# The dense expert stage in groups of four parts, two PSUM banks per operation, tokens innermost in the weights

## The chip, the core and the metric

The kernel runs on one core of a Trainium2 chip. Its engines are named as in the profile: PE multiplies matrices (PEld is its loading of the stationary operand), DVE is the vector engine, ACT the scalar engine, POOL is GpSimd, and SP issues transfers to the DMA queues. The metric is the device time of one execution in microseconds (us). One profiled execution of each kernel is looked at by the instruction; the timed runs are others.

## The reference

One layer of a streaming encoder for 1088 tokens (1024 of a prompt, 64 of a sample): three branches (an mLSTM, a gating unit, a cross-attention) are merged, and then comes a table of 16384 experts, of which every token takes 128. This last part is where the change lies:

```
def _peer(xn, w_pq, k_sub1, k_sub2, u_exp, v_exp):
    ...
        q = (xb @ w_pq).reshape(PEER_BLOCK, PEER_HEADS, PEER_DQ)
        s1 = jnp.einsum('thd,kd->thk', q[..., :half], k_sub1)
        s2 = jnp.einsum('thd,kd->thk', q[..., half:], k_sub2)
        v1, i1 = lax.top_k(s1, PEER_TOPK)
        v2, i2 = lax.top_k(s2, PEER_TOPK)
        ...
        sc, pos = lax.top_k(cand, PEER_TOPK)
        e = jnp.take_along_axis(cidx, pos, axis=-1).reshape(PEER_BLOCK, PEER_HEADS * PEER_TOPK)
        g = jax.nn.softmax(sc, axis=-1).reshape(PEER_BLOCK, PEER_HEADS * PEER_TOPK)
        a = jax.nn.gelu(jnp.einsum('tkd,td->tk', u_exp[e], xb))
        return jnp.einsum('tk,tkd->td', (g * a).astype(xb.dtype), v_exp[e])
```

Each row of `u_exp` and `v_exp` has 1024 numbers. A token's output is the sum, over its 128 experts, of weight x gelu(u . x) x v. The result is normalised (RMSNorm) and written out.

## The kernel before, in words

The 1088 tokens are nine tiles of up to 128 rows: 0 to 7 and "s". For tiles 0, 1, "s", 6 and 7 the experts are **gathered**: for each of the 128 places of a token, POOL issues one indirect DMA (L1018) that fetches one row of `u_exp` for each of 128 tokens (512 KB); DVE multiplies and sums it with the tokens (L1031, "a u row" below); the same for `v_exp` (L1039, "a v row"). There are 3 buffers for u rows and 4 for v rows (`BU, BV = 3, 4`). A gather is issued when its buffer is free, and a buffer is free when DVE has used the row ahead in it.

For tiles 2 to 5 (512 tokens, `TD`) all 16384 experts are computed **densely**. This has three stages:

- *Lookahead* (`ahead`): the four tiles are transposed to `dxh`, `dxl`, and the first `LG` = 6 parts of the hidden layer are made. A part is 256 experts: `hidden(m)` makes x . u for them and 512 tokens (L1093 to L1095, three matmuls for each product, since every operand is split in a high and a low fp32r half), and ACT puts gelu of it into `ge` (L1099).
- *Hot stage* (`dense`, L1168 to L1190): the table of weights, one number for each token and expert, is made by products of one-hot matrices, four tokens at a time: DVE compares (L1168) and multiplies (L1172), ACT scales one part of it (L1177), PE multiplies (L1181), ACT copies the 512 x 128 numbers from PSUM to a staging tile `sg` (L1183), and every 32 tokens `sg` is stored to `gd` in DRAM (L1190). Then the signal "weights" lets the selection for tiles 6 and 7 start.
- *Outer stage*: 32 steps of 512 experts. `weigh` multiplies four `ge` tiles with a piece of the weights `g4`, loaded from `gd` (L1203, L1210), casts the product to its high half (ACT, L1211) and subtracts for the low half (L1212). `outer` multiplies them with `v_exp`, 512 of 1024 columns at a time (L1223 to L1225), four PSUM banks for the four token tiles, and DVE adds each bank to `ob` in SBUF (L1229). Between the two halves of a step `hidden` runs for a part that is `LG` parts ahead.

The weights `u_exp`, `v_exp` stream through a ring: SP loads 512 KB pieces, ACT casts 512 columns to the high half (L277, in `w_split`) and DVE subtracts for the low half (L280, "a split" below). Each split serves 12 matmuls of 512 columns, in `hidden` and in `outer` alike, and is made up to four ahead (`HL` = 4).

The parts are written as Python generators, "streams", each of which yields an estimate of its cost or waits for a signal; `Flow.run` takes the stream whose sum of costs is least, and this sets the order of the code. A scheduler then sets the order on each engine. The engines run their own order strictly.

## Time and profile before

| | |
|---|---|
| timed runs | 3677.53, 3679.82, 3681.61 us (median 3679.82) |
| the profiled execution, its own time | 3696.64 us |
| its span, first to last instruction | 3694.7 us |
| PE, PEld | 3267.0 us (88%), 2635.0 us (71%) |
| DVE | 3228.9 us (87%) |
| ACT, POOL | 1381.8 us (37%), 1701.9 us (46%) |
| DMA | 1024.81 MB, 277 GB/s over the span |

A share is that of the engine's busy time in the whole span. PE's and DVE's are near each other, and a mean over the span does not say which of them waits for the other in a given stretch; the rows further down are therefore taken by stretch, in us from the start of the span.

### The profile page before, as it was taken

Reading aid. Unit: us, or ns where it says so; the run is one execution under the profiler, and the core shown is the slowest. Engines: PE = TensorE matmul, PEld = TensorE weight load, DVE = VectorE, ACT = ScalarE, POOL = GpSimd, SP = SyncE. Lnnn points to the kernel's source line nnn. Section 1 sums busy time; section 2 is a strip of 40 time slices with the busy share of each in tenths; the row PEclk is TensorE's granted clock in tenths of the full one; section 3 lists DMA queues with packets and bytes.
Section 4 is the critical chain, followed back from the end, with each engine's and each line's share of the span. In section 5 each row is a group of like instructions: output and inputs, shape, how many; then the busy total and the mean of one; then the engine's idle time right before and its main releaser. Section 6 shows DMA issues by size and latency. Waiting matters only on the chain.

```text
span 3694.7 us, 46871 instructions
## 1 busy us (share of the span) xinstructions
PE 3267.0 (88%) x15364; PEld 2635.0 (71%) x15364; DVE 3228.9 (87%) x6811; ACT 1381.8 (37%) x2671; POOL 1701.9 (46%) x1208
## 2 busy tenths in 40 slices
PE   8999998899986497599867876899999999999998
PEld 6787876576675365477756766677778888888886
DVE  5556797768989999998999899998889999999997
ACT  5555533423333143233324555332223333333332
POOL 1001334447856775654431472344345565545651
PEclk9999998899998698799978867999999999999999
DMA  7445467789897787897876797788889999999995
GB/s 231 146 163 187 158 240 253 252 278 332 320 361 277 265 300 266 287 318 270 280 256 206 232 282 238 265 286 296 294 304 354 354 350 348 344 322 317 346 338 180
DMA packets 447440, 1024.81 MB, mean 277 GB/s; under 512 B 32182, under 2 KB 169566, under 8 KB 443100
## 3 DMA queue, kind: packets, MB, share of 16 engines
q0 software_dynamic: 166528, 604.58, 46.5%
q1 hardware_dynamic: 276828, 413.06, 33.8%
q10 hardware_dynamic: 3840, 4.20, 0.4%
q8 instruction: 120, 1.97, 0.2%
q14 instruction: 124, 1.02, 0.1%
HBM read 968.44 MB, written 53.26 MB: 277 GB/s over the span
## 4 chain that ended last, share of the span: by engine, by line
PE 31%; DVE 9%; issue 7%; POOL 3%; DMA 2%; ACT 0%; DVEq 0%; POOLq 0%; ACTq 0%; SPq 0%
PE po L1225 4%; PE po L1224 4%; PE po L1223 4%; PE ph L1095 4%; PE ph L1094 4%; PE ph L1093 4%; POOL gu L1018 3%; PE po L1181 2%; DVE gacc L1039 2%; DMA gu<-in_u_exp_dram,e 1%; DVE wl L280 1%; DVE gu L1031 1%; DVE one L1172 1%; DVE ge L1210 0%; DVE one L1168 0%
## 5 line engine op out<-in xcount | busy, mean ns | idle before, releaser
L1018 POOL DMA_INDIRECT gv<-in_v_exp_dram,e x522 | 826.9, 1584 | 670.6 <-DVE gacc L1039 349.6
L1018 POOL DMA_INDIRECT gu<-in_u_exp_dram,e x576 | 746.1, 1295 | 833.5 <-DVE gu L1031 509.3
L277 ACT CAST wh<-wraw 128x512 fp32r<-128x512 f32 x994 | 612.8, 621 | 1249.6 <-PE acc L313 390.2
L1031 DVE SCALAR_TENSOR_TENSOR gu<-gu,gx 128x1024 f32<-128x1024 f32 x576 | 699.8, 1217 | 157.0 <-DMA gu<-in_u_exp_dram,e 153.2
L280 DVE TENSOR_TENSOR wl<-wraw,wh 128x512 fp32r<-128x512 f32 x962 | 651.1, 684 | 150.7 <-ACT wh L277 147.9
L1039 DVE SCALAR_TENSOR_TENSOR gacc<-gv,w,gacc 128x1024 f32<-128x1024 f32 x448 | 571.0, 1274 | 25.4 <-DMA gv<-in_v_exp_dram,e 24.1
L312 PE MATMUL acc<-wl,half 128*128 128x512 f32 (+1 forms) x1152 | 477.5, 415 | 8.3 <-DVE wl L280 8.3
L313 PE MATMUL acc<-wh,half 128*128 128x512 f32 (+1 forms) x1152 | 458.9, 404 | 0.0
L311 PE MATMUL acc<-wh,half 128*128 128x512 f32 (+1 forms) x1152 | 417.1, 413 | 6.4 <-ACT uB L470 2.6
L1224 PE MATMUL po<-wl,W 128*128 128x512 f32 x1024 | 402.4, 393 | 12.2 <-DVE wl L280 12.0
L1095 PE MATMUL ph<-dxh,wl 128*128 128x512 f32 x1024 | 393.2, 394 | 12.8 <-DVE wl L280 12.6
L1094 PE MATMUL ph<-dxl,wh 128*128 128x512 f32 x1024 | 399.7, 390 | 1.3 <-DVE dxl L1118 1.3
L1225 PE MATMUL po<-wh,W 128*128 128x512 f32 x1024 | 399.3, 391 | 0.5 <-DVE W L1212 0.5
L1093 PE MATMUL ph<-dxh,wh 128*128 128x512 f32 x1024 | 399.5, 390 | 0.2 <-ACT dxh L1117 0.2
L1223 PE MATMUL po<-wh,W 128*128 128x512 f32 x1024 | 352.4, 391 | 23.8 <-ACT W L1211 20.6
L328 PE MATMUL acc<-half,wh 128*128 128x256 f32 (+2 forms) x768 | 253.8, 350 | 18.8 <-ACT wh L277 12.5
L311 PEld LDWEIGHTS acc<-wh,half 128*128 128x128 f32 (+1 forms) x1152 | 211.8, 185 | 78.4 <-issue 15.8
L312 PEld LDWEIGHTS acc<-wl,half 128*128 128x128 f32 (+1 forms) x1152 | 214.2, 186 | 74.5 <-issue 11.4
L329 PE MATMUL acc<-half,wh 128*128 128x256 f32 (+2 forms) x768 | 261.9, 346 | 0.0
L313 PEld LDWEIGHTS acc<-wh,half 128*128 128x128 f32 (+1 forms) x1152 | 212.8, 186 | 54.7 <-issue 1.5
L330 PE MATMUL acc<-half,wl 128*128 128x256 f32 (+2 forms) x768 | 226.9, 342 | 14.7 <-DVE wl L280 14.5
L1223 PEld LDWEIGHTS po<-wh,W 128*128 128x128 f32 x1024 | 192.8, 188 | 66.0 <-ACT W L1211 20.9
(444 smaller groups left out, 5233.3 us busy)
## 6 DMA issues: line engine op xcount, KB each, us to landing
wraw<-in_w_in_dram SPq DMA_DIRECT2D x216, 512.0 KB
wraw<-in_v_exp_dram SPq DMA_DIRECT2D x125, 512.0 KB
wraw<-in_u_exp_t_dram SPq DMA_DIRECT2D x68, 512.0 KB
gd<-sg SPq DMA_DIRECT2D x16, 2048.0 KB
g<-gd SPq DMA_DIRECT2D x32, 1024.0 KB
wrawx<-in_u_exp_t_dram SPq DMA_DIRECT2D x60, 512.0 KB
wraw<-in_w_pq_dram SPq DMA_DIRECT2D x48, 512.0 KB
wraw<-in_w_out_dram SPq DMA_DIRECT2D x24, 512.0 KB
```

The costliest lines, as they stand in the source:

```text
L277: S.copy(h, t)
L280: E.tensor_tensor(l, t, h.bitcast(F32), op=ALU.subtract)
L311: T.matmul(ps[i], xh[:, cs], h, start=(k == 0), stop=False)
L312: T.matmul(ps[i], xh[:, cs], l, start=False, stop=False)
L313: T.matmul(ps[i], xl[:, cs], h, start=False, stop=(last and b is None))
L1018: G.indirect_dma_start(out=tl, out_offset=None, in_=src, in_offset=bass.IndirectOffsetOnAxis(ap=col, axis=0))
L1031: V.scalar_tensor_tensor(tl, tl, 1.0, xn, op0=ALU.mult, op1=ALU.mult, accum_out=av[:, j:j + 1])
L1039: V.scalar_tensor_tensor(x2, gt_.pop(op), st_v[t][1][:, j:j + 1], x2, op0=ALU.mult, op1=ALU.add)
L1093: T.matmul(o, h[:, cs], xh[:, k + kk, :], start=(k + kk == 0), stop=False)
L1094: T.matmul(o, h[:, cs], xl[:, k + kk, :], start=False, stop=False)
L1223: T.matmul(o, w_[:, k, cs], h, start=(k == 0), stop=False)
L1224: T.matmul(o, w_[:, k, cs], l, start=False, stop=False)
```

## The change

The constants `SC`, `NS`, `NH` go; a part is 256 experts (`NP` = 64 of them), four parts are a group (`GP` = 4), and the lookahead `LG` is 4 parts in place of 6. A PSUM tile has two banks, and one operation works on both: gelu, product, cast, subtraction and add have 1024 elements to a partition in place of 512. The outer products of four parts (1024 experts, in place of 512) are summed in PSUM ahead of one add, so 64 adds of 1024 take the place of 256 of 512. The product with the weights is made right behind each part's hidden layer (`times_g`), not all at the step's start, and `g4` is loaded after every second one into one buffer. In `gd`, `sg` and `g4` tokens are innermost, 32 in a row, in place of four experts; for this the two operands of the hot matmul change places, and one copy of 1024 elements moves 8 tokens, reading PSUM with 128 numbers between elements. `sg` lives in a pool of its own (`hp`), whose place the five `W` buffers (`vp`) take afterwards. The numbers of matmuls, splits and gathers and the bytes moved are the same. Lines of after: product L1092, hidden L1108 to L1110, equality and product L1187, L1191, hot matmul L1200, subtraction L1229, outer L1258 to L1260, add L1269.

```diff
-    gd = dram.tile([32, 128, TD, 4], F32, name="gd")
+    gd = dram.tile([32, 128, TD // 32, 4, 32], F32, name="gd")
...
-    SC = 4
-    NS = NEXP // (128 * SC)
-    LG = 6
-    NH = 4
+
+    NP = NEXP // 256
+    GP = 4
+    LG = 4
...
+    def two_banks():
+        return ps_d.tile([128, 2, 512], F32, name="po", bufs=2)
...
+    g4s = {}
+    def load_g(s_):
+        if 2 * s_ < NP:
+            g4s[s_] = dp.tile([128, TD // 32, 4, 32], F32, name="g4")
+            SP.dma_start(g4s[s_], gd[s_])
+    def times_g(m):
+        ge = st["ge", m].rearrange("p c (b t) -> p c b t", t=32)
+        g4 = g4s[m // 2].rearrange("p b c t -> p c b t")
+        V.tensor_tensor(ge, ge, g4[:, m % 2 * 2:m % 2 * 2 + 2], op=ALU.mult)
+        if m % 2:
+            g4s.pop(m // 2)
+            load_g(m // 2 + 1)
     def hidden(m):
-        if m >= 2 * NS:
+        if m >= NP:
             return
         xh, xl = st["dx"]
-        ps = [psd("ph", NH) for _ in range(2)]
+        ps = ps_d.tile([128, 2, 512], F32, name="ph", bufs=2)
         for k in range(0, KD, 2):
             h, l = w_get()
             for kk in range(2):
                 for c in range(2):
                     cs = slice(kk * 256 + c * 128, kk * 256 + c * 128 + 128)
-                    o = ps[c][:, 0:TD]
+                    o = ps[:, c, 0:TD]
                     T.matmul(o, h[:, cs], xh[:, k + kk, :], start=(k + kk == 0), stop=False)
                     T.matmul(o, h[:, cs], xl[:, k + kk, :], start=False, stop=False)
                     T.matmul(o, l[:, cs], xh[:, k + kk, :], start=False, stop=(k + kk == KD - 1))
-            yield 12 * 0.217 * TD / 512
-        for c in range(2):
-            ge = dp.tile([128, TD], F32, name="ge", bufs=2 * LG)
-            S.activation(ge, ps[c][:, 0:TD], AF.Gelu_apprx_tanh)
-            st["ge", 2 * m + c] = ge
+            yield 12 * 0.233 * TD / 512
+        ge = dp.tile([128, 2, TD], F32, name="ge", bufs=LG)
+        S.activation(ge, ps[:, :, 0:TD], AF.Gelu_apprx_tanh)
+        st["ge", m] = ge
...
-            x = dp.tile([128, D], F32, name="dxn", tag="W", bufs=2)[0:n]
+            x = dp.tile([128, D], F32, name="dxn", tag="ge", bufs=LG)[0:n]
...
-                sg = dp.tile([128, 32, 32, 4], F32, name="sg", tag="W", bufs=2)
...
+                sg = hp.tile([128, 32, 4, 32], F32, name="sg", bufs=2)
+                for t1 in range(0, 32, 8):
+                    p = two_banks()
+                    for b in range(2):
+                        tb = t0 + t1 + 4 * b
+                        ts = slice(tb, tb + 4)
+                        eq, pr = hots[tb // 4 % len(hots)]
+                        V.tensor_tensor(eq, io[:, None].to_broadcast([128, 2, 128, 4]),
+                                        kb[:, :, None, ts].to_broadcast([128, 2, 128, 4]), op=ALU.is_equal)
+
+                        nd = 2 + b
+                        V.tensor_tensor(pr[:, 0:nd], eq[:, 0, None].to_broadcast([128, nd, 128, 4]),
+                                        gb[:, 0:nd, None, ts].to_broadcast([128, nd, 128, 4]), op=ALU.mult)
+                        for j in range(nd, 3):
+                            for t2 in range(4):
+                                S.activation(pr[:, j, :, t2], eq[:, 0, :, t2], AF.Copy,
+                                             scale=gf_[:, tb + t2:tb + t2 + 1])
+
                         for t2 in range(4):
...
-                    S.copy(sg[:, :, t1:t1 + 4, :].rearrange("p g t c -> p t g c"),
-                           p.rearrange("p (t g c) -> p t g c", t=4, c=4))
-                    yield 0.7
+                            for j in range(3):
+                                T.matmul(p[:, b, t2 * 128:(t2 + 1) * 128], eq[:, 1, :, t2], pr[:, j, :, t2],
+                                         start=(j == 0), stop=(j == 2))
+                        yield 0.5
+                    S.copy(sg[:, :, :, t1:t1 + 8].rearrange("p g c t -> p (g c) t"),
+                           p.rearrange("p b (t e) -> p e (b t)", t=4))
+                    yield 0.4
                 nd1 += 32
                 if nd1 == TD:
-                    st["weights"] = sg
+                    st["weights"] = tok = kp.tile([128, 1], F32, name="tok")
+                    V.tensor_copy(tok, sg[:, 0, 0, 0:1])
                     fl.signal("weights")
-                SP.dma_start(gd[:, :, t0:t0 + 32, :].rearrange("g p t c -> p g (t c)"),
-                             sg.rearrange("p g t c -> p g (t c)"))
+                SP.dma_start(gd[:, :, t0 // 32].rearrange("g p c t -> p g (c t)"),
+                             sg.rearrange("p g c t -> p g (c t)"))
...
+        W_ = {}
+        def weigh(m):
+            if m >= NP:
+                return
+            w_ = vp.tile([128, 2, 2, TD], F32R, name="W", bufs=GP + 1)
+            ge = st.pop(("ge", m))
+            S.copy(w_[:, 0], ge)
+            V.tensor_tensor(w_[:, 1], ge, w_[:, 0].bitcast(F32), op=ALU.subtract)
+            W_[m] = w_
         load_g(0)
-        w_ = weigh(0)
+        for m in range(LG):
+            times_g(m)
+            weigh(m)
         gfin = None
         ss = dp.tile([128, 2, ND], F32, name="dss")
         V.memset(ss, 1.0)
...
+        for g in range(NP // GP):
+            last = g == NP // GP - 1
+            for j in range(2 * GP):
+                hf, q = divmod(j, GP)
+                m = GP * g + q
+                if j % 2 == 0 and GP * g + j // 2 + LG < NP:
+                    mh = GP * g + j // 2 + LG
+                    yield from hidden(mh)
+                    times_g(mh)
+                if j == 0:
+                    weigh(GP * g + LG)
+                if q == 0:
+                    ps = [two_banks() for _ in range(ND // 2)]
+                w_ = W_[m]
+                for k in range(2):
+                    h, l = w_get()
+                    for i in range(ND):
+                        o, cs = ps[i // 2][:, i % 2], slice(i * 128, i * 128 + 128)
+                        hi, lo = w_[:, 0, k, cs], w_[:, 1, k, cs]
+                        T.matmul(o, hi, h, start=(q == 0 and k == 0), stop=False)
+                        T.matmul(o, hi, l, start=False, stop=False)
+                        T.matmul(o, lo, h, start=False, stop=(q == GP - 1 and k == 1))
+                    yield 0.7 * ND
+                if hf:
+                    W_.pop(m)
+                    if q < GP - 1:
+                        weigh(GP * g + LG + q + 1)
+                if q == GP - 1:
+                    for i in range(ND // 2):
+                        o = ob[:, 2 * i:2 * i + 2, hf * 512:(hf + 1) * 512]
+                        V.tensor_tensor(o, o, ps[i], op=ALU.add)
```

How the order moves on the engines, at three places. PE, in the middle of the hot stage, where the last hidden matmul of the lookahead stands (`ph` the PSUM tile, `po` that of the hot products, `hot` a one-hot buffer). Before:

```order
L1093 MATMUL ph_19546<-dxh_16576,wh_19547 128x512
L1094 MATMUL ph_19546<-dxl_16577,wh_19547 128x512
L1095 MATMUL ph_19546<-dxh_16576,wl_19548 128x512
L1181 LDWEIGHTS hot_16690
L1181 MATMUL po_17275<-hot_16690 128x128
```

After:

```order
L1108 MATMUL ph_19271<-dxh_16576,wh_19272 128x512
L1109 MATMUL ph_19271<-dxl_16577,wh_19272 128x512
L1110 MATMUL ph_19271<-dxh_16576,wl_19273 128x512
L1200 LDWEIGHTS hot_16692
L1200 MATMUL po_17072<-hot_16692 128x128
```

Ahead of the first outer matmul PE's order has 336 hidden matmuls before (seven parts of 48, the seventh from the loop) and 240 after (five parts).

DVE, where the outer stage starts (`g_19526`, `g_19247` are the loads of the weights, `cand` and `scv` belong to the selection for tile 7). Before:

```order
L857 TENSOR_TENSOR cand<-v_15774 128x8x8
L1210 TENSOR_TENSOR ge<-ge,g_19526 128x512 x4
L857 TENSOR_TENSOR cand<-v_15774 128x8x10
L857 TENSOR_TENSOR cand<-v_15774 128x8x12
L857 TENSOR_TENSOR cand<-v_15774 128x8x8
L981 COPY gx_22592<-gacc 64x1024
L1212 TENSOR_TENSOR W<-ge,W 128x512 x3
L799 MAX scv<-cand 128x8 x2
L1031 SCALAR_TENSOR_TENSOR gu,av<-gu,gx 128x1024
L799 MAX scv<-cand 128x8
```

After:

```order
L1092 TENSOR_TENSOR ge<-ge,g_19247 128x1024 x2
L897 TENSOR_TENSOR ei<-ei,oh 128x256
L1229 TENSOR_TENSOR W<-ge,W 128x1024
L906 SCALAR_TENSOR_TENSOR e<-ei 128x128
L857 TENSOR_TENSOR cand<-v_15774 128x8x16
L857 TENSOR_TENSOR cand<-v_15774 128x8x8
L857 TENSOR_TENSOR cand<-v_15774 128x8x10
L857 TENSOR_TENSOR cand<-v_15774 128x8x12
L857 TENSOR_TENSOR cand<-v_15774 128x8x8
L1229 TENSOR_TENSOR W<-ge,W 128x1024
L981 COPY gx_22009<-gacc 64x1024
L799 MAX scv<-cand 128x8 x8
L1092 TENSOR_TENSOR ge<-ge,g_19254 128x1024 x2
```

The products come in pairs of twice the size; the second pair, of the second load, stands 10 rows behind the first.

DVE further on, in the stretch of tile 6's u rows. Before:

```order
L1229 TENSOR_TENSOR ob<-ob,po 128x512 x4
L280 TENSOR_TENSOR wl<-wraw,wh 128x512
L1031 SCALAR_TENSOR_TENSOR gu,av<-gu,gx 128x1024
L280 TENSOR_TENSOR wl<-wraw,wh 128x512
L1031 SCALAR_TENSOR_TENSOR gu,av<-gu,gx 128x1024 x2
L280 TENSOR_TENSOR wl<-wraw,wh 128x512 x2
L1031 SCALAR_TENSOR_TENSOR gu,av<-gu,gx 128x1024
L1210 TENSOR_TENSOR ge<-ge,g_21750 128x512
L1031 SCALAR_TENSOR_TENSOR gu,av<-gu,gx 128x1024
L280 TENSOR_TENSOR wl<-wraw,wh 128x512
L1210 TENSOR_TENSOR ge<-ge,g_21750 128x512
L280 TENSOR_TENSOR wl<-wrawx,wh 128x512
```

After:

```order
L280 TENSOR_TENSOR wl<-wraw,wh 128x512
L1031 SCALAR_TENSOR_TENSOR gu,av<-gu,gx 128x1024
L280 TENSOR_TENSOR wl<-wraw,wh 128x512
L1092 TENSOR_TENSOR ge<-ge,g_20914 128x1024
L1031 SCALAR_TENSOR_TENSOR gu,av<-gu,gx 128x1024
L280 TENSOR_TENSOR wl<-wrawx,wh 128x512
L1031 SCALAR_TENSOR_TENSOR gu,av<-gu,gx 128x1024
L280 TENSOR_TENSOR wl<-wrawx,wh 128x512
L1031 SCALAR_TENSOR_TENSOR gu,av<-gu,gx 128x1024
L280 TENSOR_TENSOR wl<-wraw,wh 128x512
L1269 TENSOR_TENSOR ob<-ob,po 128x2x512 x2
L1031 SCALAR_TENSOR_TENSOR gu,av<-gu,gx 128x1024
```

Four adds of one bank in a row become two of two banks, in every second step, and one product of 1024 takes the place of two. Counted from the first product on, the 34th u row stands behind 43 splits before and behind 39 after; the 128th behind 132 and behind 120. Up to the 34th there are 24 products, 16 subtractions and 20 adds before, and 9, 9 and 4 after. From the first to the last equality operation of the hot stage there are 24 splits before and 17 after, and 64 v rows in both.

## Rows read from the trace of the kernel before

**Rows 1.** The profile page, part 1: busy time of each engine, its share of the span, and its instructions.

```profile
PE 3267.0 (88%) x15364; PEld 2635.0 (71%) x15364; DVE 3228.9 (87%) x6811; ACT 1381.8 (37%) x2671; POOL 1701.9 (46%) x1208
```

**Rows 2.** Busy time of each engine in four stretches. Columns: the stretch in us, its length, then busy us (and instructions) of PE, PE's weight loads, DVE, ACT and POOL, the granted TensorE clock, the share of the DMA engines, GB/s.

```profile
2150.00:2200.00 50.00, 34.25 (x275) 30.62 (x274) 49.08 (x64) 28.12 (x69) 36.01 (x16) 0.63 0.87 276
2550.00:2600.00 50.00, 47.39 (x204) 37.54 (x203) 43.20 (x70) 14.28 (x25) 20.60 (x18) 1.00 0.87 297
2900.00:2950.00 50.00, 50.00 (x223) 41.40 (x222) 50.00 (x70) 15.17 (x26) 29.22 (x23) 1.00 0.98 355
3655.00:3668.00 13.00, 13.00 (x59) 10.78 (x58) 8.01 (x22) 3.49 (x6) 0.00 (x0) 1.00 0.37 135
```

**Rows 3.** The timeline of PE, at two places of the dense stage: start, length, engine, line, instruction, out<-in. Each row is one matmul of 512 columns; rows between are left out.

```profile
3449.53 0.39 PE L1093 MATMUL ph<-dxh,wh 128*128 128x512 f32 x1
...
3450.43 0.39 PE L1094 MATMUL ph<-dxl,wh 128*128 128x512 f32 x1
...
3655.41 0.39 PE L1223 MATMUL po<-wh,W 128*128 128x512 f32 x1
...
3656.09 0.39 PE L1223 MATMUL po<-wh,W 128*128 128x512 f32 x1
```

**Rows 4.** PE's instructions by line from 2317.7 us to 3682 us: count, busy us, mean ns, and the idle time before them with what ended it.

```profile
L1093 PE MATMUL ph<-dxh,wh 128*128 128x512 f32 x912 | 355.8, 390 | 0.0
...
L1223 PE MATMUL po<-wh,W 128*128 128x512 f32 x1024 | 352.4, 391 | 23.8 <-ACT W L1211 20.6 <-DVE ob L1229 3.1
```

**Rows 5.** The timeline where the outer products begin (SPq is the queue that issues transfers on SyncE).

```profile
2297.14 0.58 ACT L1183 COPY sg<-po 128x512 f32<-128x512 f32 x1 [0.83 <-PE po L1181]
...
2297.75 0.40 SPq L1190 DMA_DIRECT2D gd<-sg  x1
...
2310.91 0.32 SPq L1203 DMA_DIRECT2D g<-gd  x1
...
2315.97 3.07 DVE L1210 TENSOR_TENSOR ge<-ge,g 128x512 f32<-128x512 f32 x3 [3.17 <-DMA g<-gd]
...
2317.74 0.80 PE L1223 MATMUL po<-wh,W 128*128 128x512 f32 x1 [20.63 <-ACT W L1211]
```

**Rows 6.** The timeline at the last outer matmul.

```profile
3681.02 0.39 PE L1225 MATMUL po<-wh,W 128*128 128x512 f32 x1
```

**Rows 7.** The waits from 2360 to 2760 us: engine and line, what it waited for, total us, times, longest.

```profile
POOL gu L1018 <- DVE gu L1031: 204.8, 111, 7.0
...
DVE gu L1031 <- DMA gu<-in_u_exp_dram,e: 43.4, 43, 3.2
...
PE ph L1095 <- DVE wl L280: 11.7, 16, 2.2
```

**Rows 8.** The timeline of DVE: the 34th gathered row of tile 6 (2450.90), a product and the split behind it, a split, the 128th row (2720.14) and the split behind it.

```profile
2450.90 1.22 DVE L1031 SCALAR_TENSOR_TENSOR gu<-gu,gx 128x1024 f32<-128x1024 f32 x1
...
2560.49 1.09 DVE L1210 TENSOR_TENSOR ge<-ge,g 128x512 f32<-128x512 f32 x1
2561.49 0.69 DVE L280 TENSOR_TENSOR wl<-wraw,wh 128x512 fp32r<-128x512 f32 x1
...
2719.54 0.69 DVE L280 TENSOR_TENSOR wl<-wraw,wh 128x512 fp32r<-128x512 f32 x1
2720.14 1.22 DVE L1031 SCALAR_TENSOR_TENSOR gu<-gu,gx 128x1024 f32<-128x1024 f32 x1
...
2721.29 0.69 DVE L280 TENSOR_TENSOR wl<-wraw,wh 128x512 fp32r<-128x512 f32 x1
```

**Rows 9.** DMA issues of the u gathers, from 2450 to 2700 us and from 500 to 700 us: count, and median us from issue to landing.

```profile
gu<-in_u_exp_dram,e POOLq DMA_INDIRECT x86, 6.5
...
gu<-in_u_exp_dram,e POOLq DMA_INDIRECT x74, 5.6
```

**Rows 10.** DVE's instructions by line from 2450.8 to 2721.28 us.

```profile
L1031 DVE SCALAR_TENSOR_TENSOR gu<-gu,gx 128x1024 f32<-128x1024 f32 x95 | 115.8, 1221 | 37.3 <-DMA gu<-in_u_exp_dram,e 36.6
```

**Rows 11.** The same from 500 to 700 us.

```profile
L1031 DVE SCALAR_TENSOR_TENSOR gu<-gu,gx 128x1024 f32<-128x1024 f32 x74 | 90.2, 1220 | 41.0 <-DMA gu<-in_u_exp_dram,e 40.9
```

**Rows 12.** The timeline of the hot stage: the last hidden matmul of the lookahead, the 33rd equality operation, four scaled copies of ACT, the last product.

```profile
2083.28 0.40 PE L1095 MATMUL ph<-dxh,wl 128*128 128x512 f32 x1
...
2101.03 0.68 DVE L1168 TENSOR_TENSOR hot<-one 128x1024 bf16<-128x1024 bf16 x1
...
2291.97 1.48 ACT L1177 ACTIVATE one<-one,hot 128x128 bf16<-128x128 bf16 x4
...
2293.78 0.95 DVE L1172 TENSOR_TENSOR gu<-gu,one 128x1536 bf16<-128x1536 bf16 x1
```

**Rows 13.** DVE's instructions by line from 1990 to 2101 us.

```profile
L1168 DVE TENSOR_TENSOR one<-one 128x1024 bf16<-128x1024 bf16 x16 | 11.0, 689 | 6.1 <-PE po L1181 6.1
...
L1168 DVE TENSOR_TENSOR gu<-one 128x1024 bf16<-128x1024 bf16 x8 | 5.5, 690 | 2.9 <-PE po L1181 2.9
```

**Rows 14.** ACT's instructions by line from 2100 to 2250 us.

```profile
L1183 ACT COPY sg<-po 128x512 f32<-128x512 f32 x65 | 40.1, 620 | 30.9 <-PE po L1181 30.7
```

**Rows 15.** DVE's instructions by line from 2315.9 to 2450.9 us.

```profile
L1031 DVE SCALAR_TENSOR_TENSOR gu<-gu,gx 128x1024 f32<-128x1024 f32 x34 | 41.1, 1213 | 3.7 <-DMA gu<-in_u_exp_dram,e 3.7
L1210 DVE TENSOR_TENSOR ge<-ge,g 128x512 f32<-128x512 f32 x24 | 24.9, 1066 | 3.2 <-DMA g<-gd 3.2
L280 DVE TENSOR_TENSOR wl<-wraw,wh 128x512 fp32r<-128x512 f32 x31 | 20.9, 680 | 0.0
```

More of the change, by code (lines that the diff above doesn't have):

```diff
@@ L611, in tile_stream_step @@
         want_u(m)
-    for m in range(2 * NS):
-        want_u(m + LG)
-        s_, hf = divmod(m, 2)
-        for r in range(2):
-            e0 = s_ * 128 * SC + 256 * r
+    for g in range(NP // GP):
+        for j in range(2 * GP):
+            if j % 2 == 0:
+                want_u(GP * g + j // 2 + LG)
+            hf, q = divmod(j, GP)
+            e0 = (GP * g + q) * 256
             pieces.append(a["v_exp"][e0:e0 + 256, hf * 512:(hf + 1) * 512].rearrange("(k p) c -> p k c", p=128))
@@ L1126, in dense @@
         yield "dx"
+        hot = ExitStack()
+        hp = hot.enter_context(tc.tile_pool(name="hp", bufs=1))
         one = dp.tile([128, 5 * TD + 512 + 2 * 2560], BF, name="one", tag="ob")
@@ L1131, in dense @@
         io = one[:, 5 * TD:5 * TD + 512].rearrange("p (c t) -> p c t", t=4)
[L1132 removed]
+        ioi = hp.tile([128, 128, 4], I32, name="ioi", tag="sg", bufs=2)
         G.iota(ioi, pattern=[[1, 128], [0, 4]], base=0, channel_multiplier=0)
@@ L1192, in dense @@
         yield "ahead"
+        hot.close()
+        vp = pool("vp", 1)
         ob = dp.tile([128, ND, D], F32, name="ob")
@@ L1197, in dense @@
             SP.dma_start(ob[0:n, i, :], x2d[t])
-        gs = {}
-        def load_g(s_):
-            if s_ < NS:
-                gs[s_] = dp.tile([128, TD, 4], F32, name="g4")
-                SP.dma_start(gs[s_], gd[s_])
-        def weigh(s_):
-            w_ = dp.tile([128, SC, 2 * TD], F32R, name="W", bufs=2)
-            g4 = gs.pop(s_)
-            for ci in range(SC):
-                ge = st.pop(("ge", SC * s_ + ci))
-                V.tensor_tensor(ge, ge, g4[:, :, ci], op=ALU.mult)
-                S.copy(w_[:, ci, 0:TD], ge)
-                V.tensor_tensor(w_[:, ci, TD:], ge, w_[:, ci, 0:TD].bitcast(F32), op=ALU.subtract)
-            load_g(s_ + 1)
-            return w_
-        def outer(s_, hf, w_):
-            ps = [psd("po", ND) for _ in range(ND)]
-            for k in range(SC):
-                h, l = w_get()
-                for i, t in enumerate(DENSE):
-                    o, cs = ps[i], slice(i * 128, i * 128 + 128)
-                    lo = w_[:, k, TD + i * 128:TD + 128 + i * 128]
-                    T.matmul(o, w_[:, k, cs], h, start=(k == 0), stop=False)
-                    T.matmul(o, w_[:, k, cs], l, start=False, stop=False)
-                    T.matmul(o, lo, h, start=False, stop=(k == SC - 1))
-                yield 0.65 * ND
-            for i in range(ND):
-                o = ob[:, i, hf * 512:(hf + 1) * 512]
-                V.tensor_tensor(o, o, ps[i], op=ALU.add)
+        W_ = {}
[7 more added lines that the diff above has]
+            W_[m] = w_
         load_g(0)
-        w_ = weigh(0)
+        for m in range(LG):
+            times_g(m)
+            weigh(m)
         gfin = None
@@ L1235, in dense @@
         V.memset(ss, 1.0)
-        for s_ in range(NS):
-            for q in range(2):
-                yield from hidden(2 * s_ + q + LG)
-                yield from outer(s_, q, w_)
-                if s_ == NS - 1:
-                    if gfin is None:
-                        gfin = gain(dp, "g_final", name="gfin", tag="W", bufs=2)
-                    for i, t in enumerate(DENSE):
-                        n = ROWS_OF[t]
-                        cs = slice(q * 512, q * 512 + 512)
-                        jk = dp.tile([128, 512], BF, name="djk", tag="ge", bufs=2 * LG)
-                        S.activation(jk[0:n], ob[0:n, i, cs], AF.Square, accum_out=ss[0:n, q, i:i + 1])
-                elif q == 1:
-                    w_ = weigh(s_ + 1)
+        for g in range(NP // GP):
+            last = g == NP // GP - 1
+            for j in range(2 * GP):
+                hf, q = divmod(j, GP)
+                m = GP * g + q
[25 more added lines that the diff above has]
+                        V.tensor_tensor(o, o, ps[i], op=ALU.add)
+                    if last:
+                        if gfin is None:
+                            gfin = gain(dp, "g_final", name="gfin", tag="ge", bufs=LG)
+                        for i, t in enumerate(DENSE):
+                            n = ROWS_OF[t]
+                            cs = slice(hf * 512, hf * 512 + 512)
+                            jk = dp.tile([128, 512], BF, name="djk", tag="ge", bufs=LG)
+                            S.activation(jk[0:n], ob[0:n, i, cs], AF.Square, accum_out=ss[0:n, hf, i:i + 1])
```

27 lines of the change are left out of this document (4 added, 23 removed).

## The prediction

> **What bounds the kernel now.** I read the page's busy line and 40 slices first, then the busy time by stretch, the instructions one by one in the stretches that decide, and last the waits. The page alone leaves two candidates, PE with 88% and DVE with 87% of the span [rows 1]. By stretch the dense part splits in three [rows 2]. Up to about 2318 us the hot products are made; there DVE is full (49.08 of 50 us in 2150:2200) and PE is not (34.25). From 2318 to about 2760 neither is full (2550:2600: PE 47.39, DVE 43.20). From then to the end PE works without a gap, 50.00 of 50, and DVE is nearly as full in most of it (50.00).
>
> Which of the two is the limit there? Four matmuls of 512 columns start in a row in 0.90 us from 3449.53 on, 0.225 each, and three in 0.68 us from 3655.41 on, 0.2267 each, where DVE has only 8.01 of 13 us to do [rows 2, 3]. The 223 of 2900:2950 give 0.2242, the same within the rounding. I take 0.2267. As the pace is the same with DVE full and with DVE light, it is PE's own. So from 2760 us on DVE time given back is worth nothing, and only the number of matmuls left counts.
>
> From the first outer matmul to the last, 2317.74 to 3681.02, there are 3 x 1024 outer and 3 x 912 hidden ones, 5808 [rows 4 to 6]: 5808 x 0.2267 = 1316.7 of 1363.7 us. So 47 us are lost, nearly all between 2318 and 2760. Who loses them is in the waits of that stretch: POOL waits 204.8 us for DVE to give back one of three u buffers, DVE waits 43.4 us for gathered rows to land, and PE waits for splits behind DVE [rows 7]. It is a ring of three buffers: 94 gathers go from 2450.90 to 2720.14, 2.86 us each, each landing 6.5 us after its issue; early in the kernel, where a landing takes 5.6 us, 74 gathers took 200 us, 2.70 each [rows 8, 9, 11]. DVE idles 36.6 us of the first of these on landings alone [rows 10], so a freer DVE would hardly speed the ring.
>
> **The change, part by part.**
> *Lookahead.* Ahead of the first outer matmul PE's order now holds 240 hidden matmuls, not 336. The 96 others move behind it, where PE is the limit: 96 x 0.2267 = +21.8 us. This is the largest term, and it is arithmetic on the order.
>
> *Hot stage.* What they leave behind is time in which PE is partly idle. PE's hidden parts end at 2083.28, and until 2101 DVE waits for PE on the products' buffers (L1168, 6.1 and 2.9 us) [rows 12, 13]. Without 21.8 us of PE work that wait goes, and DVE has 7 splits fewer to make, 7 x 0.60 = 4.2 us (one split, start to start, is 2719.54 to 2720.14 [rows 8]). The rest is DVE's own work, unchanged: the equality and product operations keep their number and size. 4.2 and about 8 of the waits give 12 us, at least 4 (the splits alone), at most 20 (nearly all of the 21.8). Then the chain to the first outer matmul is the old one: last copy 2297.14, store from 2297.75, load of g at 2310.91, first product 2315.97, first matmul 2317.74 [rows 5]. The product and cast are twice as large, +1 us. I take **-11 us** (-20 to -4).
>
> *The copies to the staging tile.* 64 copies of 1024 elements replace 128 of 512, and now read PSUM with 512 bytes from one element to the next. No row shows such a read. Below, the bound is a 1024-element ACT operation at twice the 620 ns of a copy, 1.2 us; above, four times that. From the 33rd equality at 2101.03 to the last product at 2293.78, DVE makes 192 us of work for 48 times 8 tokens, 4.0 us each; ACT's four scaled copies of 8 tokens take 1.48 us [rows 12, 14]; so a copy costs nothing up to 2.5 us. I take the low end, as the old copy already wrote scattered 16-byte pieces at 620 ns.
> [...]
>
> *Larger operations on DVE.* Per 512 experts DVE made 8 adds, 4 subtractions at 0.60 and 4 products at 1.00 (2560.49 to 2561.49), 11.2 us; now it makes 6 operations of 1024 elements at about 1.2, from the u product's 1.15 start to start, 7.1 us [rows 8]. So 4 us per 43.5 us of PE work are saved, some 129 us in all. In the gap-free stretch that is worth nothing, since PE's own matmuls cover it; without that cover it is rival (b)'s price.
>
> *The ring stretch.* In DVE's order the 34th gathered row of tile 6 stood behind 43 splits and the 128th behind 132; now they stand behind 39 and 120. Before, these 132 splits, each of 12 matmuls or 2.72 us, are 359 us of PE work in the 404 us from 2315.97 to 2720.14: 45 lost. Now: up to the 34th row DVE is full, with 134.9 us from 2315.97 to 2450.90, for 43 splits, 24 products, 20 adds and 16 subtractions (counted in the order) beside the rows and the selection, with 7 us idle [rows 15]; the order now has 39 splits, 9 products, 4 adds and 9 subtractions, the last three twice as large: -2.4, -13.2, -7.2 and +1.2 us, 113. With 4 us for the second load of g4, which stands close at the start, 117. Then 94 rows on the ring, at the mean of 2.70 and 2.86: 2.78 x 94 = 261. Together 378 us after the first product, with 120 x 2.72 = 326 us of PE work: 52 lost, **+7 us** (-1 at 2.70, +14 at 2.86). So the freed DVE time is not filled: the order has fewer splits for PE in the time that the ring takes anyway.
>
> *The rest at nothing.* The single g4 buffer is loaded after every second product. A load took 5 us (2310.91 to 2315.97) and has 21.8 us of PE work until it is wanted, in the gap-free stretch; at the start, where it stands close, its 4 us are in the 117 above, and PE has then 48 matmuls in hand, 10.9 us. Matmul counts, bytes moved and gathers are the same. The two-bank tiles give as many partial sums as before, and the add of one half lies under the 48 hidden matmuls that follow, 10.9 us against 2.4. The last add is 0.5 us longer, behind the last matmul.
>
> **Sum:** -11 + 21.8 + 7 + 0.5 = **+18 us**. The profiled execution took 3696.64 us (span 3694.7), 0.46% over the median of the timed runs, 3679.82; against that median it is **3698 us**.
>
> **The rivals.**
> (a) *The ring runs faster* because a less loaded DVE gives a buffer back sooner. At 2.5 us a gather, 235 us replace 261 and with them 26 of loss: 18 - 26 = -8, so 3672 and, with the hot stage at its best, 3663. For it: POOL's 204.8 us of waiting ends on DVE. Against it: at 6.5 us to land, three buffers cannot go round in under (6.5 + 1.2)/3 = 2.57 us.
> (b) *DVE is the limit of the gap-free stretch.* Then 4 us go in each of 21 times 43.5 us, 84 us in all: 3614; or 3650 if DVE is it for part of them. Against it stands the pace with DVE light [rows 3]. [...]
> (c) *No change.* The hot stage gives back all of the 21.8 us, and the ring runs at 2.70: -20 + 21.8 - 1 = +1, 3681; half of either is still inside 0.2%, up to 3687.
> (d) *The strided copy is slow.* At 4.8 us, ACT needs 6.3 us for 8 tokens against DVE's 4.0: 64 x 2.3 = +147; at 3 us 64 x 0.5 = +32. Then 3730 to 3845. For it: 512 bytes between elements is farther than any stride in this trace's copies. Against it: ACT has 2.5 us for each, from which on it decides.
>
> **How the numbers follow.** No change can be told from 3672.5 to 3687.2 us, 0.2% of the median to either side. Chances: the forecast 0.50 (its own range 3688 to 3712), (c) 0.25, (a) 0.13, (b) 0.05, (d) 0.07. The range takes in (c) and the near half of (a), and above the upper ends of the hot stage and the ring (-4, +14: 3712), with a little for the start: 3664 to 3718. Faster: 0.18, (a) and (b). Same: 0.26. Slower: 0.56.
>
> **What would show it.** Right: 240 hidden matmuls before the first outer one, that one at 2305 to 2312 us; the profile from about 2800 us on with PE at 50.00 of 50 and DVE at some 45; 94 rows of tile 6 in 255 to 270 us; copies under 2 us. Wrong: hidden and outer matmuls closer than 0.2267 us (b); gathers under 2.6 us apart (a); ACT full and DVE waiting for it in the hot stage (d); the first outer matmul before 2300 us (c). New waits would show as PE waiting for W or for an add, or DVE for g4.

## The result, and the profile after

The changed kernel takes 3709.93 us (median of 3708.15 to 3719.21) against 3680.72 us of the kernel before on the same chip: 1.0083 times as long, 95% interval 1.0063 to 1.0104. It is slower by 29 us; 18 were forecast, and the time lies in the range.

The page of the changed kernel, part 1, with the columns of [rows 1]:

```profile
PE 3282.1 (89%) x15364; PEld 2636.0 (71%) x15364; DVE 3104.9 (84%) x6492; ACT 1364.1 (37%) x2477; POOL 1668.7 (45%) x1208
```

DVE gave back 124 us, near the 129 worked out for its larger operations, and PE got 15 us busier with the same number of matmuls. Busy time by stretch, columns as in [rows 2]:

```profile
2150.00:2200.00 50.00, 37.47 (x301) 34.86 (x301) 50.00 (x65) 29.29 (x61) 38.30 (x16) 0.73 0.91 281
...
2550.00:2600.00 50.00, 45.87 (x190) 35.33 (x189) 37.25 (x56) 13.00 (x20) 22.44 (x18) 0.98 0.84 285
...
2900.00:2950.00 50.00, 50.00 (x219) 40.85 (x218) 44.24 (x56) 15.90 (x23) 25.64 (x21) 1.00 0.95 342
...
3650.00:3690.00 40.00, 40.00 (x172) 31.87 (x171) 11.20 (x15) 9.91 (x20) 0.00 (x0) 1.00 0.13 40
```

The three stages stand as before: DVE full, then neither full, then PE full. But look at the counts of the third. In 2900:2950 PE is full in both kernels at the same granted clock of 1.00, and does 219 matmuls where it did 223 [rows 2]. Which ones are slower is seen by line, here from 2800 to 3500 us; of the kernel before:

```profile
L1225 PE MATMUL po<-wh,W 128*128 128x512 f32 x519 | 202.0, 389 | 0.0
...
L1095 PE MATMUL ph<-dxh,wl 128*128 128x512 f32 x512 | 195.5, 389 | 0.0
```

and of the changed one:

```profile
L1260 PE MATMUL po<-wh,W 128*128 128x512 f32 x507 | 201.0, 396 | 0.0
...
L1110 PE MATMUL ph<-dxh,wl 128*128 128x512 f32 x505 | 196.6, 389 | 0.0
```

The hidden matmul takes 389 ns in both, the outer one 396 in place of 389. From start to start, the mean over some 1700 pairs of 2800 to 3600 us is 0.2267 us for both kinds before; after, it is 0.2269 for hidden and 0.2342 for outer ones. That is no contention with DVE: at the end, where DVE is busy 11.20 of 40 us, the pace is the same, 9 steps in 2.11 us (timeline of PE in the changed kernel):

```profile
3654.61 0.39 PE L1258 MATMUL po<-wh,W 128*128 128x512 f32 x1
...
3656.72 0.40 PE L1258 MATMUL po<-wh,W 128*128 128x512 f32 x1
```

The chain's two ends and the ring, from the timeline of the changed kernel:

```profile
1954.68 0.80 PE L1108 MATMUL ph<-dxh,wh 128*128 128x512 f32 x1 [1.43 <-DVE dxl L1132]
...
2287.78 0.76 PE L1258 MATMUL po<-wh,W 128*128 128x512 f32 x1 [20.62 <-ACT W L1228]
...
2409.12 1.23 DVE L1031 SCALAR_TENSOR_TENSOR gu<-gu,gx 128x1024 f32<-128x1024 f32 x1 [1.52 <-DMA gu<-in_u_exp_dram,e]
...
2670.83 1.22 DVE L1031 SCALAR_TENSOR_TENSOR gu<-gu,gx 128x1024 f32<-128x1024 f32 x1
...
3693.74 0.40 PE L1260 MATMUL po<-wh,W 128*128 128x512 f32 x1
```

The first phase is the same program in both, and its length differs from run to run: the first hidden matmul stands at 1969.05 in the trace of before and at 1944 to 1957 us in four others with the same first phase. Its profiled execution was 16 us over the median, and this is where they lie. So I compare from the first hidden to the last outer matmul, "the dense part": 1969.05 to 3681.02 [rows 6], 1712.0 us before, and 1739.1 us after. The difference, 27.1 us, and 1.0 at the end (from the last matmul to the end of the span 13.7 before, 14.7 after) make 28, near the 29 of the timed runs. A dense part is one execution's: it was 1711.2 and 1711.6 us in two more traces of the unchanged dense order, and 1735.6 in a second one of the changed kernel (below).

### The profile page after: what moved, and what is told of

Same layout as the page of the kernel before. It is cut to its first block, busy times and chain, and to the rows that moved or that the text cites. A ratio compares the mean times of both kernels' runs of the same rounds, so it can differ in the third digit from the quotient of the medians.

```text
span 3708.4 us, 46240 instructions
## 1 busy us (share of the span) xinstructions
PE 3282.1 (89%) x15364; PEld 2636.0 (71%) x15364; DVE 3104.9 (84%) x6492; ACT 1364.1 (37%) x2477; POOL 1668.7 (45%) x1208
## 4 chain that ended last, share of the span: by engine, by line
PE 33%; DVE 8%; issue 6%; POOL 3%; DMA 3%; ACT 0%; DVEq 0%; POOLq 0%; ACTq 0%
PE po L1259 5%; PE po L1260 5%; PE po L1258 5%; PE ph L1110 5%; PE ph L1108 5%; PE ph L1109 5%; POOL gu L1018 3%; DVE gacc L1039 2%; PE po L1200 1%; DMA gu<-in_u_exp_dram,e 1%; DMA gv<-in_v_exp_dram,e 1%; DVE one L1191 1%; DVE one L1187 1%; PE acc L330 0%; PE acc L328 0%
## 5 line engine op out<-in xcount | busy, mean ns | idle before, releaser
L1018 POOL DMA_INDIRECT gv<-in_v_exp_dram,e x522 | 797.1, 1527 | 648.9 <-DVE gacc L1039 335.8
L312 PE MATMUL acc<-wl,half 128*128 128x512 f32 (+1 forms) x1152 | 474.7, 413 | 6.4 <-DVE wl L280 6.4
L313 PE MATMUL acc<-wh,half 128*128 128x512 f32 (+1 forms) x1152 | 457.9, 403 | 0.0
L1258 PE MATMUL po<-wh,W 128*128 128x512 f32 x1024 | 403.0, 397 | 20.6 <-ACT W L1228 20.6
L1110 PE MATMUL ph<-dxh,wl 128*128 128x512 f32 x1024 | 403.6, 394 | 19.9 <-DVE wl L280 19.9
L1260 PE MATMUL po<-wh,W 128*128 128x512 f32 x1024 | 406.3, 397 | 0.0
L1108 PE MATMUL ph<-dxh,wh 128*128 128x512 f32 x1024 | 401.4, 392 | 1.4 <-DVE dxl L1132 1.4
L312 PEld LDWEIGHTS acc<-wl,half 128*128 128x128 f32 (+1 forms) x1152 | 212.7, 185 | 71.3 <-issue 11.3
L313 PEld LDWEIGHTS acc<-wh,half 128*128 128x128 f32 (+1 forms) x1152 | 211.6, 185 | 55.0 <-issue 2.1
L1110 PEld LDWEIGHTS ph<-dxh,wl 128*128 128x128 f32 x1024 | 193.2, 189 | 70.4 <-DVE wl L280 30.3
```

Source lines behind the costliest of these rows:

```text
L312: T.matmul(ps[i], xh[:, cs], l, start=False, stop=False)
L313: T.matmul(ps[i], xl[:, cs], h, start=False, stop=(last and b is None))
L1018: G.indirect_dma_start(out=tl, out_offset=None, in_=src, in_offset=bass.IndirectOffsetOnAxis(ap=col, axis=0))
L1110: T.matmul(o, l[:, cs], xh[:, k + kk, :], start=False, stop=(k + kk == KD - 1))
L1258: T.matmul(o, hi, h, start=(q == 0 and k == 0), stop=False)
L1260: T.matmul(o, lo, h, start=False, stop=(q == GP - 1 and k == 1))
```

## The experiments

Four causes for the slow outer matmul were open: where W lies in SBUF relative to `wh` and `wl` (the five W buffers now follow two small tiles, `dss` of 32 bytes and one of 64), how high it lies, the two-bank PSUM tiles, and the sums over eight steps. All pads below leave every engine's order as it is. The distances are those from a `wh` buffer to a `W` buffer, in bytes, as the built programs place them; the pace is the outer matmul's mean from start to start over 700 to 800 us of the gap-free stretch, the few steps over 0.3 us left out:

```
kernel                        distance   past a multiple of 256   outer, us   dense part, us
before                           49152               0             0.2267        1712.0
changed                          94304              96             0.2342        1739.1
changed, W +32  (e1_w_even)      94336             128             0.2325        1736.5
before,  W +32  (e2_w_odd)       49184              32             0.2332        1732.1
changed, W +416 (e5_w512)        94720               0             0.2267        1716.5
before,  W +256 (e7_w256)        49408               0             0.2267        1711.2
```

**W moved by 32 bytes in the changed kernel**

```diff
-        ss = dp.tile([128, 2, ND], F32, name="dss")
+        ss = dp.tile([128, 2, 8], F32, name="dss")[:, :, 0:ND]
```

> The changed kernel with one tile of its outer stage 32 bytes larger, so that the five W buffers start at a multiple of 64 bytes in SBUF, as the wh and wl buffers do there; in the changed kernel W starts 32 bytes past one and wh and wl at one, in the kernel before all of them 32 bytes past. Theory A (the outer matmul, 0.2342 us from start to start in the changed kernel against 0.2267 before, is slow because its stationary and its moving operand lie in different halves of 64 bytes): 0.227 us again, 3072 x 0.0075 = 23 us less, about 3687 us. Theory B (it is slow because of the two-bank PSUM tiles or the sums over eight steps) and theory C (because W lies higher in SBUF): 0.234 us still, about 3710 us.

1.0078 (1.0050 to 1.0106), and 0.2325 us in place of 0.2342: nearly nothing. The theory in this form, halves of 64 bytes, falls, and so does a measure of 128 bytes, since this distance is a multiple of 128.

**W moved by 32 bytes in the kernel before**

```diff
-        xl = dp.tile([128, KD, TD], F32R, name="dxl")
+        xl = dp.tile([128, KD * TD + 8], F32R, name="dxl")[:, 0:KD * TD].rearrange("p (k t) -> p k t", k=KD)
```

> The kernel before with one tile 32 bytes larger, so that W starts at a multiple of 64 bytes while wh, wl, dxh and dxl stay 32 bytes past one. Everything else is the kernel before, its order too. Theory A: the outer matmul slows from 0.2267 to about 0.234 us, the hidden one stays, 23 us more, about 3704 us. Theories B and C: no change, about 3681 us.

1.0056 (1.0035 to 1.0077), with one-bank tiles, sums over four steps and W at its old height. By line, 2800 to 3500 us:

```profile
L1225 PE MATMUL po<-wh,W 128*128 128x512 f32 x503 | 198.8, 395 | 0.0
...
L1095 PE MATMUL ph<-dxh,wl 128*128 128x512 f32 x512 | 195.8, 390 | 0.0
```

So the place of W alone makes the outer matmul slow, 0.2332 us in place of 0.2267, and PSUM, the sums and the height are not needed for it. Here the pace is in the time as well: 0.56% is 21 us, and the dense part is 20 us longer.

**W at a multiple of 512 bytes, in the changed kernel**

```diff
-        ss = dp.tile([128, 2, ND], F32, name="dss")
+        ss = dp.tile([128, 2, 56], F32, name="dss")[:, :, 0:ND]
```

> The changed kernel with one tile of its outer stage 416 bytes larger, so that W starts 185 x 512 bytes behind wh; in the kernel before this distance is 96 x 512 bytes, in the changed one it is 184 x 512 and 96 bytes more. Theory A' (two operands of a matmul must lie a multiple of 512 bytes apart, the length of a stationary row; 32, 96 and 128 bytes past one gave 0.233, 0.234 and 0.2325 us): the outer matmul at 0.227 us, from the first hidden to the last outer matmul 1739 - 23 = 1716 us in place of the changed kernel's 1739 and the 1712 of before, and 6 us over the kernel before in time. Theories B and C (PSUM tiles, sums over eight steps, place high in SBUF), on what distance does not explain: still 0.232 us or more, 1737 us.

The dense part takes 1716.5 us, as expected, and the outer matmul 0.2267 (by line 389 ns, 2800 to 3500 us):

```profile
L1260 PE MATMUL po<-wh,W 128*128 128x512 f32 x517 | 201.1, 389 | 0.0
```

This W begins at a multiple of 256, as the slow W of the run before (140288) does: it is not W's own address but its distance. The timed runs recover far less than the trace: 6 us over the kernel before were expected, and they are at 1.0061 (1.0038 to 1.0085), 22 us over it.

**W 256 bytes further, in the kernel before** (as in the second run, with 64 numbers in place of 8)

> The kernel before with W 256 bytes further from wh, nothing else. Theory A' with 512 as the measure: the outer matmul slow, 0.23 us or more. If 256 (or 64) bytes are the measure: 0.2267 us.

0.2267 us, and 1.0004 (0.9993 to 1.0016) in time. 512 falls too: of the measures tried 256 bytes is left, since 128 past one was slow in the first run.

**The changed kernel and the moved W on one chip**

> The changed kernel itself once more, on the same chip as the next two: its time against the kernel before, and a second trace. 0.8% slower, and from the first hidden to the last outer matmul 1739 us again, with the outer matmul at 0.234 us.

> The changed kernel with W 185 x 512 bytes behind wh once more, beside the changed kernel on one chip. Its trace gave 1716.5 us from the first hidden to the last outer matmul, its timed runs 0.6% over the kernel before. If the 22.5 us of the trace are in the time, it is 0.6% faster than the changed kernel here; if they are lost elsewhere, the two are the same.

1.0069 (1.0042 to 1.0096) and 1.0047 (1.0026 to 1.0068): about 8 us apart, with intervals that overlap, not 23. The second traces keep the two paces, 0.2342 and 0.2267 us, but their dense parts do not differ: 1735.6 us for the changed kernel (1739 expected), 1735.4 for the moved W. Counted from the 2401st matmul of the dense part on, at about 2830 us, the changed kernel takes 864.1 and 868.0 us in its two traces, the moved W 849.3 and 851.8: behind the ring the pace is in both pairs, 15 to 16 us. Ahead of it the changed kernel takes 875.0 and 867.7, the moved W 867.2 and 883.6. So 16 of the 19 us that the moved W's second trace lost against its first lie ahead of that mark, nearly all of them in the ring's stretch. First the trace with 1716.5 us, then this one, by stretch:

```profile
2300.00:2400.00 100.00, 95.53 (x412) 77.84 (x411) 90.48 (x207) 32.95 (x47) 49.01 (x34) 0.98 0.88 304
```

```profile
2300.00:2400.00 100.00, 89.75 (x371) 72.26 (x370) 80.32 (x203) 31.40 (x45) 57.65 (x30) 0.95 0.81 273
```

PE does 41 matmuls fewer in 100 us, is 6 us less busy, and its granted clock is 0.95 in place of 0.98. In steps of 20 us, eight of this trace's 23 from 2300 to 2760 show a clock under 0.95, two in the changed kernel's first trace. All lie in the stretch in which PE waits for splits; PE is busy 16.7 to 18.3 of 20 us in them. Which of the two traces is the usual one is not shown. Taking each matmul at its pace, PE loses 44 to 51 us behind the first outer one in every other trace with three u buffers, and 66 in this one; but of the 19 timed executions with W moved, the one traced first had the highest mean granted clock, 0.928, where the others had 0.922 to 0.927. So the part of the 23 us that the ring takes back in the timed runs stays open.

**The lookahead alone**: the kernel before with `LG = 4`.

> The kernel before with a lookahead of four parts in place of six, and nothing else. My step: 96 matmuls x 0.2267 = 21.8 us move behind the first outer matmul, and that one comes about 10 us earlier: 11 us more, about 3692 us. Rival: the hot stage gives back all of the 21.8 us, 3681 us. Other rival: it gives back nothing, 3702 us.

The first outer matmul stands 334.5 us behind the first hidden one, 348.7 before: 14.2 earlier. The dense part is 1721.5 us, 9.5 longer. In time 1.0006 (0.9983 to 1.0030), 2 us where 11 were expected, which does not tell 9 us from none; the trace bears the term out, the timed runs do not show it.

**The lookahead back at six, W at a multiple of 256, four W buffers**

```diff
-    LG = 4
+    LG = 6
...
-            w_ = vp.tile([128, 2, 2, TD], F32R, name="W", bufs=GP + 1)
+            w_ = vp.tile([128, 2, 2, TD], F32R, name="W", bufs=GP)
...
-                if j == 0:
-                    weigh(GP * g + LG)
...
-                    if q < GP - 1:
-                        weigh(GP * g + LG + q + 1)
+                    weigh(GP * g + GP + q)
```

> The run with W at a multiple of 512 bytes, and the lookahead back at six parts; the 8 KB for it come from W, which has four buffers in place of five, each made again when its last product is out. Lookahead term as in the sum: 96 matmuls, 21.8 us, go back ahead of the first outer matmul, which then comes about 14 us later. From the first hidden to the last outer matmul 1716 - 22 + 14 = 1708 us, so 3 to 4 us faster than the kernel before. If five W buffers were needed, PE would wait for W and lose some of it: 1715 or more.

0.9997 (0.9977 to 1.0016): with the lookahead and the distance both put back, the whole loss is gone. How it divides between the two in time is not shown: this run and the moved W with four parts were timed on one chip, 1.0061 against 0.9997, while their traces have dense parts of 1716.5 and 1715.7 us, less than 1 us apart. The dense part is 7 us over the expectation: the first outer matmul comes 348.4 us behind the first hidden one, 3 more than I took, and some 5 us are waits for splits between 3293 and 3321 us. PE's waits from 2760 us on:

```profile
PE ph L1110 <- DVE wl L280: 3.9, 3, 1.7
```

No wait for W is among them.

**Four u buffers**: the run with six parts, with `LG = 5` and

```diff
-    BU, BV = 3, 4
+    BU, BV = 4, 4
```

> As the run with six parts, but with five, and the 4 KB so freed given to a fourth buffer for u rows (in the first phase too). If the ring of three buffers, 6.5 us to land, sets the 45 us that PE loses from the first outer matmul to the 128th u row: a row in (6.5 + 2.3) / 4 = 2.2 us in place of 2.8, so 94 rows take 55 us less, and of the loss 10 to 20 us are left: from the first hidden to the last outer matmul 1716 - 11 + 7 - 30 = 1682 us, and some 30 us faster than the kernel before. If landings grow as the gathers come closer: 1712, and no gain.

0.9822 (0.9805 to 0.9838), 66 us faster than before where 30 were expected, and the best kernel here. The dense part is 1665.7 us, 46 less than before (1682 expected), and the first hidden matmul stands at 1920.8: the rest comes from the first phase, which has the same ring. By stretch, where the changed kernel had 37 to 47 us of DVE and 45 to 48 of PE:

```profile
2350.00:2400.00 50.00, 50.00 (x223) 41.39 (x222) 47.62 (x84) 14.03 (x21) 24.05 (x22) 1.00 0.97 365
...
2500.00:2550.00 50.00, 50.00 (x223) 41.39 (x221) 42.96 (x68) 15.01 (x23) 25.76 (x21) 1.00 0.96 342
```

PE is full in the ring's stretch, and the clock stays at 1.00. All waits of PE in its outer stage:

```profile
PE ph L1110 <- DVE wl L280: 3.4, 3, 1.7
```

94 rows take 223.5 us, 2.38 each (2.2 expected). Of the 51 us that PE lost behind the first outer matmul in the run with six parts, 7 are left, so with the larger operations the ring of three is the cause of nearly all of it.

**Four u buffers in the kernel before** (`LG = 5`, `BU, BV = 4, 4`)

> The kernel before with four u buffers in place of three, and a lookahead of five parts to make room for the fourth; all else as before, its small operations too. My reading of the ring: the 45 us lost from 2318 to 2720 us shrink as they did with the larger operations (7 us left there). If the DVE time that the change saves is worth nothing here as well, from the first hidden to the last outer matmul 1712 + 4 - 38 = 1678 us, and some 60 us faster than before. If DVE becomes the limit where the rows come 2.2 us apart (43 of 50 us busy at 2.86 us apart), some of the loss stays: 1690 us or more, and 40 us faster.

0.9873 (0.9847 to 0.9898), a dense part of 1696.5 us: the second case. 94 rows take 250.2 us there, and PE still loses 33 us, against 47 with three buffers. By stretch DVE is busier than in the run above, and PE has gaps again:

```profile
2400.00:2450.00 50.00, 46.87 (x205) 37.95 (x204) 48.19 (x86) 14.98 (x26) 25.70 (x20) 1.00 0.90 309
...
2550.00:2600.00 50.00, 47.54 (x203) 38.84 (x202) 46.63 (x77) 14.08 (x25) 26.48 (x21) 0.97 0.93 330
```

So the larger operations with W at a good distance, worth nothing behind a ring of three (0.9997), are worth about 0.5% behind a ring of four (0.9822 against 0.9873). The two were timed on different chips, each against the kernel before.

**Four u buffers and W at its slow distance**: the run with four u buffers, with `dss` as the changed kernel has it, 96 bytes past a multiple of 256.

> The run with four u buffers and the larger operations, with W back at 96 bytes past a multiple of 512 from wh, as the changed kernel has it, and nothing else different. There PE hardly waits from the first outer matmul on, so what the pace of the outer matmuls costs is seen in the time without the ring's waits beside it: 0.234 us in place of 0.2267, 3072 x 0.0075 = 23 us, so 1689 us from the first hidden to the last outer matmul in place of 1665.7, and 1.2% faster than the kernel before in place of 1.8%. If the distance costs nothing in time: 1.8% again.

0.9873 (0.9848 to 0.9897) in place of 0.9822; the dense part 1691.0 in place of 1665.7 us, 25 more. By line, 2800 to 3500 us:

```profile
L1259 PE MATMUL po<-wh,W 128*128 128x512 f32 x512 | 202.9, 396 | 0.0
```

Where few ring waits lie beside it, the distance is in the time too: 0.5%, some 19 us. That is as much as the larger operations are worth there: with W at the slow distance they end where the kernel before does with four buffers, 0.9873.

**The same in the first phase**

```diff
-    ones4 = mp.tile([36, 1], F32, name="ones4")
+    ones4 = mp.tile([36, 16], F32, name="ones4")[:, 0:1]
```

> The kernel before with one small tile of the first phase 32 bytes larger, so that the operands half and mT of the projections lie 32 bytes past a multiple of 64, as wh and wl do; before they lie at one. Theory A, carried to the first phase, where these matmuls of 512 columns start 0.233 us apart in both kernels: 0.227 us there, 3456 x 0.006 = 21 us less where all of them are the limit, half of it if half are: 3660 to 3670 us. If A does not hold there: 3681 us.

1.0001 (0.9980 to 1.0023). The mean from L312 to L313 went from 0.2330 to 0.2294 us: two of the three `half` buffers now lie a multiple of 256 from `wh`, the third and `mT` do not. The pace follows the distance, as far as it was changed. The time does not show it; its interval leaves room for 7 us.

## Why the prediction was right, and where its sum was not

*The bound.* Right. The gap-free stretch is PE's: DVE fell from 50.00 to 44.24 of 50 us there and bought nothing. Rival (b) is out: with W at a good distance PE keeps 0.2267 us with the lighter DVE (e5).

*The lookahead, +21.8.* Right in the traces: 240 hidden matmuls stand ahead of the first outer one, and in the kernel before with four parts (e3) the stretch from the first to the last outer matmul is 23.7 us longer.

*The hot stage, -11 (-20 to -4).* The first outer matmul stands 333.1 us behind the first hidden one, 348.7 before: -15.6, and -14.2 for the lookahead alone (e3). Right within its bounds, 3 to 5 us too small. With the lookahead alone the parts are near those I named: from the first equality operation to the last product 12.9 us less (12 said), and no change in the chain behind. In the changed kernel that stretch is only 9.1 us shorter, since of the waits of DVE's equality operations for PE, 12.3 us before (6.1, 3.3 and 2.9), 8.2 are left (1960 to 2290 us):

```profile
DVE one L1187 <- PE po L1200: 5.1, 9, 0.7
...
DVE gu L1187 <- PE po L1200: 2.2, 3, 0.7
```

The chain behind is 0.8 longer (1 said), and the first equality operation comes 7.3 us nearer to the first hidden matmul, which I had not counted. Rival (c) needed -20. The sign named for it was badly chosen: I had given an absolute time, 2305 to 2312 us, and before 2300 for rival (c). The matmul stands at 2287.78, since the first phase of this execution was 14 us shorter; only the distance from the first hidden matmul can be compared.

*The strided copies, nothing.* Right. ACT's row from 1960 to 2280 us:

```profile
L1203 ACT COPY sg<-po 128x1024 f32<-128x1024 f32 x64 | 65.5, 1023 | 88.5 <-PE po L1200 88.4
```

1023 ns for 1024 numbers, against 2 x 620 [rows 14], and ACT waits 88.5 us for PE ahead of these copies. Rival (d) is out; its 4.8 us were my guess at an upper bound. This read of PSUM, 512 bytes from one element to the next, took as long as the gelu's read of 1024 numbers that lie in a row in PSUM (L1113), 1022 ns on average. The product with its weights in runs of 32 takes 1220 ns for 1024 numbers, against 2 x 1066 with the weights 16 bytes apart [rows 15].

*The ring, +7.* Its pace was right: the 34th row at 2409.12, 123.8 us behind the first product (117 said), the 128th at 2670.83, so 94 rows in 261.7 us, 2.78 each (2.78 said). Rival (a) is out. But PE's loss did not grow. Taking each kind at its own pace, 2832 x 0.2267 + 3072 x 0.2342 = 1361.5 us of the 1406.0 from 2287.78 to 3693.74 are work, 44.5 lost; 47 before. That is -2.5, outside the bounds of -1 to +14. I had stopped counting at the 128th row. Up to it, by the same count, PE lost 34.8 us before and 40.9 after, 6 more, near the 7 forecast (37.0 in the second trace of the changed kernel); behind it 12.0 before and 3.8 after (7.5). (The 45 lost up to that row was counted by the splits in DVE's order, and PE was further on by then.) In 2700:2750 and 2750:2800 of the kernel before PE is not full:

```profile
2700.00:2750.00 50.00, 43.77 (x184) 34.15 (x184) 42.12 (x66) 12.73 (x24) 23.08 (x19) 1.00 0.87 307
2750.00:2800.00 50.00, 49.37 (x205) 40.60 (x206) 49.60 (x73) 15.52 (x27) 29.59 (x21) 0.93 0.94 332
```

and of the changed kernel it is, from 2700 us on:

```profile
2700.00:2750.00 50.00, 50.00 (x219) 40.80 (x218) 48.92 (x63) 15.06 (x23) 32.60 (x26) 1.00 1.02 389
```

*The step that failed* is one sentence of the first part: "As the pace is the same with DVE full and with DVE light, it is PE's own." It is PE's own, but it is not the same for every placement of its operands: 0.2267 us before, 0.2342 after. I carried 0.2267 us over to tiles that the change puts elsewhere, and costed "the two-bank tiles" at nothing without asking where the small tiles ahead of the W buffers push them. That is 3072 x 0.0075 = +23.0 us of PE's work. W moved alone shows it in the kernel before (20 us in the dense part, 21 in time) and with four u buffers (25 and 19); in the changed kernel itself the first pair of traces shows 22.5, the second none, and the time 8 with overlapping intervals.

The sum as measured in the two first traces: -15.6 + 21.8 - 2.5 + 23.0 + 1.0 = +28. Mine: -11 + 21.8 + 7 + 0.5 = +18. Two terms were too high, by 5 and by 9.5 us, and one of 23 was not seen. That the time still fell in the range is partly luck: by these traces the change without the slow distance is worth +5, which I had called no change. The timed runs with W moved are 17 to 22 us over the kernel before, near my 18, so whether the forecast would have held without the distance is open.

## What to carry to other kernels

Compare the pace of the same matmul in two traces, by line and in starts per stretch, before any argument on waits: a full engine can be slower, as PE was here with 219 matmuls in 50 us in place of 223. When a change moves tiles, print where the operands of the hot matmuls lie, and keep the stationary and the moving one a multiple of 256 bytes apart: an outer matmul took 0.2267 us so here, and 0.2325 to 0.2342 at the four other distances tried; two tiles of 32 and 64 bytes in a pool ahead of W were enough here to lose 3% of the outer matmul's pace, and so were 32 bytes more in one tile of the kernel before. And work saved on an engine that waits for a ring of buffers was worth nothing here until the ring had one more: the fourth buffer was worth 1.3% in the kernel before and 1.8% with the larger operations, which it made pay.

## What the runs showed of the hardware that was not expected

- A 512-column fp32r matmul starts every 0.2267 us when its two operands lie a multiple of 256 bytes apart in SBUF (six placements: 49152, 49408, 94720, 98816, 102912 for outer ones, 16384 for hidden ones), and every 0.2325 to 0.2342 us when they lie 32, 96 or 128 bytes past one (four). Distances past a multiple of 256 other than these were not tried for outer matmuls, and why it is so no run shows.
- A read of PSUM by ACT with 512 bytes between elements ran at 1.0 ns an element (1023 ns for 1024), as fast as the gelu's read of elements in a row (1022 ns for 1024). The old copy took 616 ns for 512, and the old gelu 600; so one larger operation in place of two saves some 200 ns with either.
- With the order fixed, the length of the first phase differs by 25 us between profiled executions (first hidden matmul at 1944 to 1969 us), so a difference of 10 us is better read between two marks in a trace than from the ends. Even so one trace is not enough: between the same two marks, two executions of one program took 1716.5 and 1735.4 us.
